# Two transformer blocks: score matmuls with all 128 rows, modulation in three MLPs, the softmax's factor on ScalarE

## The chip, the cores and the metric

The kernel runs on one core of one Trainium2 chip. The metric is the device time of one execution in microseconds. Three runs of the kernel before took 3540.41, 3541.93 and 3547.73 us; the median, 3541.93, is what a change is compared with. The engines are TensorE (PE in the profile, its weight loads PEld), VectorE (DVE), ScalarE (ACT), GpSimd (POOL) and SyncE (SP), which issues the DMAs.

## The reference

Two blocks of two layers each act on x, 512 tokens of 1024 channels, in float32. A layer of the first block, cut:

```python
u = rms_norm(h, attn_norm[l])
proj = u @ w_in[l]          # dq dk dv rq rk rv rg gq gk gv gate_logits
dq, dk = partial_rope(rms_norm(dq)), partial_rope(rms_norm(dk))
a = rms_norm(differential_attention(dq, dk, dv, lam), diff_subln[l]) * (1 - lambda_init)
r = silu(rg) * head_group_norm(bidirectional_retention(rq, rk, rv, ...))
gq, gk = axial_rope(rms_norm(gq)), axial_rope(rms_norm(gk))
c = grouped_query_attention(gq, gk, gv)
merged = sum over the three of sigmoid(gate) * (branch @ w_branch[l])
h = h + merged @ w_out[l]
h = h + square(relu(rms_norm(h, mlp_norm[l]) @ w_mlp_in[l])) @ w_mlp_out[l]
```

Differential attention has 4 heads, each with two softmaxes over 64 channels; the grouped attention has 8 query heads and 2 key heads of 64 channels. A layer of the second block, which also has a context stream ctx of 256 tokens:

```python
mx = split(silu_c  @ w_mod[l] + b_mod[l], 6)      # silu_c of c, for x
mc = split(silu_cc @ w_mod[l] + b_mod[l], 6)      # of c_ctx, for ctx
zx = (rms_norm(x, norm1_g[l]) * (1 + mx[1]) + mx[0]) @ w_in[l]   # zc from ctx alike
# queries of x (8 heads, 96 channels) attend to the 768 keys of ctx and x; in layer 0 ctx attends to its own 256
x = x + mx[2] * (concat(fourier, attention, conv) @ w_o[l])
x = x + mx[5] * (square(relu(modulate(rms_norm(x, norm2_g[l]), mx[3], mx[4]) @ w_mlp1[l])) @ w_mlp2[l])
# layer 0: the same for ctx with mc; layer 1: ctx is used for keys and values alone
return rms_norm(x, final_norm_g)
```

So of layer 1's modulation the context needs the first two of the six parts (columns 0 to 15 of 48 blocks of 128), and x all six.

## The kernel before

Activations lie transposed, 128 channels in the partitions and tokens in the free dimension, in tiles of 512 columns (256 for the context). Every operand of a matmul is split into a high part in fp32r and a low part, the rest, so a product is two or three matmuls (`mm3`, `gemm`). Weights come as blocks of 128x1024 (`wload`): SP loads one into a `raw` tile (3 of them), ScalarE writes the high part into a `w` tile, VectorE subtracts for the low part (`lo`, the rows `w<-raw,w`). There are 6 `w` tiles. The tag `r` holds 512-column fp32r tiles, 40 of them and some more in a phase (X1 in the first block's mixer).

The program runs phase after phase: for each of two layers of the first block the mixer (`mixer1`) and then the output projection and the MLP; then for each of two layers of the second block `mixer2` and its projection and MLP. In the trace of before the stretches are about 0 to 560 and 1000 to 1545 us for `mixer1`, 560 to 1000 and 1545 to 1965 for the first two MLPs, 1965 to 2260 and 2870 to 3140 for `mixer2`, 2260 to 2870 and 3140 to 3537 for the last two MLPs.

No code gives the order in which instructions stand in the engines' queues. `Sched` records the operations of a phase and then runs a list scheduler on them with a table of costs (`_cost`): each engine takes the ready operation with the smallest priority, which is its place in the record less a bonus (`sc.ahead`). A tile is taken when an operation starts and given back after its last reader. What comes out is a fixed order for each engine; the hardware works through each queue in order.

The scores of the first block (`scores`): the 64 channels of a query head lie stacked, the high part in one half of the partitions and the low part in the other (`stack_queries`). `stack_keys` writes the key's high part into both halves, with ScalarE and a copy on VectorE, and its low part into one half on GpSimd. The first matmul of a score tile then has 128 rows, high and low queries times high keys; the second has the 64 rows of the high queries times the low keys:

```python
mm(ps, q[m][:, a], k[0][m], True, False)
mm(ps, q[m][rows[m], a], k[1][rows[m]], False, True)
```

The softmax (`softmax`) takes the minimum on VectorE (the scores carry a minus sign), the exponential and its sum on ScalarE, and the reciprocal on VectorE. Then GpSimd multiplies the tile `e` by the reciprocal, TensorE transposes it, and ScalarE and VectorE split it into the parts for the product with the values. This stands three times: in `diff_attend` (of two softmaxes the first alone), `gqa_attend` and, for the second block, in `attend` inside `mixer2`.

The modulation vectors of the second block are computed beside the MLPs of the first (`side`, `modulation`). For each of 48 blocks of 128 outputs SP loads 128x1024 of the weights into an `mraw` tile (3 of them), and VectorE multiplies by the row silu(c) and sums, once for x and once for the context. Layer 0's 96 passes run in the first MLP, layer 1's 64 in the second. `mlp` calls `next(side)` after every second unit of its first half and after every unit of its second half; the scheduler may take these operations whenever tiles are free.

Of the kernel before, what the change touches and what calls it, by code (L numbers as in the profile page):

```python
# [21 lines left out]
D = 1024  # L22
T = 512
# [12 lines left out]
NRAW = 3  # L36
X1 = 8
X2 = 1
# [20 lines left out]
YADD = "V"  # L59
HALVES = 'P'  # L60
SWAP8 = list(range(8, 16)) + list(range(8)) + list(range(16, 32))
SWAP16 = list(range(16, 32)) + list(range(16))
# [69 lines left out]
class Op:  # L132
    __slots__ = ("eng", "calls", "cost", "prio", "idx", "bufs", "deps", "nexts", "ready", "unstarted", "soon", "allocs", "frees", "done", "rel", "outs", "port")

# [15 lines left out]
class Sched:  # L150


    def __init__(self, tc):
        self.tc, self.nc = tc, tc.nc
        self.tags, self.ops, self.bufs, self.bias, self.macro = {}, [], [], 0.0, None
        self.behind, self.dma, self.port = {}, 0.0, 0.0
        nc = tc.nc
        self.engines = {"PE": nc.tensor, "DVE": nc.vector, "ACT": nc.scalar, "POOL": nc.gpsimd, "SP": nc.sync}
# [60 lines left out]
    def ahead(self, n):  # L219
# [3 lines left out]
        self.bias = old  # L223

    def record(self, eng, name, a, k):
        call = (eng, name, a, k)
        if self.macro is not None:
            self.macro.append(call)
        else:
            self._add([call])  # L230

    def _add(self, calls):
# [16 lines left out]
        for b, r in writes:  # L249

            deps.update((o.idx, o) for o, q in b.written if starts or _meet(q, r))
            deps.update((o.idx, o) for o, q in b.read if _meet(q, r))
        op.deps = list(deps.values())
        op.prio = op.idx + self.bias
        op.allocs, op.frees = [], []
# [15 lines left out]
    def run(self):  # L271
# [44 lines left out]
        port = self.port  # L316
        events, order, now, dma = [(t, 0, 0) for t in sorted({0.0, *free_at.values()})], [], 0.0, self.dma
        for op in ops:
            if not op.done:
                if op.ready:  # L320
# [53 lines left out]
        while left:  # L374
# [30 lines left out]
            while events and events[0][0] <= now:  # L405
# [15 lines left out]
                for n in op.nexts:  # L421
                    n.done -= 1
                    n.ready = max(n.ready, now + lag(op, n))
                    if not n.done:
                        if n.ready <= now:
# [10 lines left out]
            while finished[low]:  # L436
                low += 1
            for t in self.tags.values():
                if t.blocked:
                    wake(t)  # L440
# [82 lines left out]
def kernel(  # L523
# [346 lines left out]
    def mixer1(l, mp, u):  # L870
# [86 lines left out]
        def stack_keys(x):  # L957

            out, l_ = [], sc.alloc("r")
            for r, o in zip(rows, reversed(rows)):  # L960
                k = sc.alloc("r")
                S.activation(k[r], x[r], AF.Copy)
                V.tensor_copy(k[o], k[r])
                lo(l_[r], x[r], k[r], G)
                out.append(k)
            return out, l_

        def scores(q, k, m, qt):

            a = slice(qt * P, (qt + 1) * P)  # L970
            ps = psum("sc")
            with sc.group():
                mm(ps, q[m][:, a], k[0][m], True, False)
                mm(ps, q[m][rows[m], a], k[1][rows[m]], False, True)
            return ps
# [61 lines left out]
        def diff_attend(hd, q, k, v, bo):  # L1037
            acc = psum("acc")
            for half in range(2):
                pt = [pair(T), pair(T)]  # L1040
                for j in range(2):
                    es = [sc.alloc("e") for m in range(2)]
                    r0, r1 = (softmax(scores(q, k, m, half * 2 + j), es[m]) for m in range(2))
                    V.tensor_tensor(out=r1, in0=r1, in1=neglam, op=ALU.mult)
                    G.tensor_scalar(out=es[0], in0=es[0], scalar1=r0, scalar2=0.0, op0=ALU.mult, op1=ALU.add)
                    V.scalar_tensor_tensor(out=es[0], in0=es[1], scalar=r1, in1=es[0], op0=ALU.mult, op1=ALU.add)
# [82 lines left out]
        def gqa_attend(i, q, k, v, out):  # L1129
            y = t32()  # L1130
            for m in range(2):
                acc = psum("acc")
                r = rows[m]
                for half in range(2):
                    pt = [pair(T), pair(T)]
                    for j in range(2):
                        e = sc.alloc("e")
                        rs = softmax(scores(q, k, m, half * 2 + j), e)
                        G.tensor_scalar(out=e, in0=e, scalar1=rs, scalar2=0.0, op0=ALU.mult, op1=ALU.add)
                        to_pt(e, pt, j)  # L1140
                        if j:
                            pv2(acc, v[m], pt, half)
                        yield
# [91 lines left out]

    mod = {(l, x): fixed(gp, 48, f"mod{l}{x}") for l in range(L) for x in "xc"}
    kept_c = {x: sc.fixed(dram.tile([P, D], F32, name=f"silu{x}")) for x in "xc"}

    def modulation(l):

        row = {}
        for i, x in enumerate("xc"):
            row[x] = sc.alloc("mrow")
            if l == 0:
                c, g = sc.alloc("mraw"), row[x]
                SP.dma_start(c, cc_d[i])
                S.activation(g, c, AF.Tanh, scale=0.5)
# [5 lines left out]
        yield  # L1253
        for j in range(48):
            who = "xc" if l == 0 or j < 16 else "x"
            raw = sc.alloc("mraw")
            SP.dma_start(raw, wmod_d[l, j])
            for x in who:
                out = raw if x == who[-1] else sc.alloc("junk")
                V.scalar_tensor_tensor(out=out, in0=raw, scalar=1.0, in1=row[x], op0=ALU.mult, op1=ALU.mult,  # L1260
                                       accum_out=mod[l, x][:, j:j + 1])
            yield
        for x in "xc":
            n = 48 if l == 0 or x == "x" else 16
            m = mod[l, x]
            V.tensor_tensor(out=m[:, :n], in0=m[:, :n], in1=vec[:, COL[f"bm{l}"]:COL[f"bm{l}"] + n], op=ALU.add)
            for at, g in ((8, f"n1{l}"), (32, f"n2{l}")):
                if at < n:
                    V.scalar_tensor_tensor(out=m[:, at:at + 8], in0=m[:, at:at + 8], scalar=1.0,
# [6 lines left out]
    def mixer2(l, mp, ux, uc):  # L1276
# [193 lines left out]
        def attend(v, y, par, si):  # L1470
# [5 lines left out]
            for hf in range(nq // 256):  # L1476
                pt = [pair(T) for _ in range(nk // 256)]
                for j in range(2):
# [261 lines left out]
    def side(l):  # L1740
        if l == 1:
            yield from context()
        yield from modulation(l)

# [42 lines left out]
    for l in range(L):  # L1787
        with phase(f"m2{l}", B2,
# [177 lines left out]
```

## Time and profile before

| | us |
|---|---|
| median of three runs | 3541.93 (3540.41 to 3547.73) |
| the profiled execution | 3539.29 |
| its span in the trace | 3537.5 |
| busy: PE, DVE, ACT, POOL | 3348.9, 2285.2, 1437.4, 948.2 |
| granted TensorE clock, mean | 0.977 of full speed |

The span is from the first to the last instruction of the program in one profiled execution; 1.8 us lie around it. Busy time is the time in which an engine has an instruction running; matmuls are pipelined, so that the length of one is longer than the time until the next can start. Nearly all operations are issued from one line of the kernel, so groups are told apart by the names of their tiles: `e<-sc,s` reads a score tile and writes an exponential. "issue" as what an engine waited for means nothing that the trace shows. The rows themselves stand in their own section below.

### The profile page before, as it was taken

How to read it: one execution, taken by the hardware profiler on the slowest of the kernel's cores; microseconds unless marked ns; L12 is line 12 of the kernel's file. 1: busy time of each engine (PE TensorE's matmuls, PEld its weight loads, DVE VectorE, ACT ScalarE, POOL GpSimd, SP SyncE). 2: the span in 40 equal slices, each digit the busy share in tenths (PEclk: the TensorE clock that was granted, in tenths of full speed). 3: DMA queues.
4: the chain of work that ended last, by engine and by line, in shares of the span. 5: the costliest groups of instructions: out<-in, count | busy, mean ns of one | idle time of the engine just before them, and what ended most of it. 6: DMA issues, size and time to landing. Idle time of an engine off the chain costs nothing.

```text
span 3537.5 us, 46905 instructions
## 1 busy us (share of the span) xinstructions
PE 3348.9 (95%) x17724; PEld 2823.5 (80%) x17724; DVE 2285.2 (65%) x4048; ACT 1437.3 (41%) x2699; POOL 948.2 (27%) x886
## 2 busy tenths in 40 slices
PE   6999999999989999999999987899999988889998
PEld 6787778788877877778888776788888886878887
DVE  7787866897378878668733898552332369963334
ACT  4554443322345544443223466441221334743233
POOL 4222323211132223231101565220210235621002
PEclk9999999999999999999999999999999998999999
DMA  3121124464321112154723210211111221022222
GB/s 125 60 69 60 66 72 173 154 213 162 110 97 55 69 66 72 66 179 159 270 99 104 69 37 1 84 60 59 61 68 58 69 79 50 19 84 96 96 96 84
DMA packets 100307, 324.48 MB, mean 92 GB/s; under 512 B 11120, under 2 KB 18288, under 8 KB 100080
## 3 DMA queue, kind: packets, MB, share of 16 engines
q1 hardware_dynamic: 100080, 321.48, 26.9%
q8 instruction: 139, 2.28, 0.3%
q14 instruction: 88, 0.72, 0.1%
HBM read 312.00 MB, written 9.44 MB: 91 GB/s over the span
## 4 chain that ended last, share of the span: by engine, by line
PE 85%; DVE 9%; ACT 3%; issue 2%; POOL 1%; DMA 0%; SPq 0%; DVEq 0%; ACTq 0%; POOLq 0%
PE mm L447 79%; PE sc L447 5%; DVE r L447 2%; DVE h L447 2%; PE acc L447 2%; DVE w L447 1%; DVE s L447 1%; DVE t L447 1%; ACT r L447 1%; ACT e L447 1%; DMA raw<-in_win_dram 0%; ACT t L447 0%; ACT w L447 0%; POOL t L447 0%; POOL h L447 0%
## 5 line engine op out<-in xcount | busy, mean ns | idle before, releaser
L447 PE MATMUL mm<-r,w 128*128 128x512 f32 (+1 forms) x12134 | 2570.7, 363 | 55.1 <-DVE w L447 23.0
L447 PEld LDWEIGHTS mm<-r,w 128*128 128x128 f32 x12134 | 2041.9, 191 | 399.7 <-DVE w L447 26.2
L447 DVE TENSOR_TENSOR w<-raw,w 128x1024 fp32r<-128x1024 f32 (+1 forms) x466 | 588.0, 1268 | 736.4 <-issue 358.1
L447 ACT ACTIVATE w<-raw 128x1024 fp32r<-128x1024 f32 (+1 forms) x466 | 483.7, 1046 | 1042.1 <-PE mm L447 900.8
L447 POOL TENSOR_SCALAR e<-e,s 128x512 f32<-128x512 f32 (+1 forms) x176 | 158.1, 901 | 397.6 <-DVE s L447 377.7
L447 ACT ACTIVATE e<-sc,s 128x512 f32<-128x512 f32 (+2 forms) x208 | 153.5, 739 | 131.5 <-DVE s L447 130.0
L447 PE MATMUL mm<-rc,w 128*128 128x256 f32 x768 | 166.1, 281 | 0.0
L447 DVE TENSOR_REDUCE s<-sc 128x1 f32<-128x512 f32 (+2 forms) x208 | 152.5, 741 | 19.3 <-PE sc L447 18.9
L447 PEld LDWEIGHTS mm<-rc,w 128*128 128x128 f32 x768 | 139.8, 189 | 20.3
L447 POOL TENSOR_TENSOR t<-t,t 128x512 f32<-128x512 f32 (+2 forms) x72 | 92.4, 1285 | 189.5 <-DVE t L447 162.9
L447 PE MATMUL mm<-r,r 128*128 128x256 f32 (+1 forms) x595 | 125.5, 343 | 11.5 <-DVE r L447 6.1
L447 DVE SCALAR_TENSOR_TENSOR mraw<-mraw,mrow 128x1024 f32<-128x1024 f32 x96 | 129.8, 1362 | 4.4 <-DMA mraw<-in_wmod_dram 3.1
L447 POOL TENSOR_TENSOR x<-t,x 128x512 fp32r<-128x512 f32 (+1 forms) x58 | 82.5, 1425 | 175.1 <-ACT x L447 175.1
L447 ACT ACTIVATE r<-mm 128x256 fp32r<-128x256 f32 (+1 forms) x278 | 98.0, 401 | 63.1 <-PE mm L447 60.0
L447 DVE SCALAR_TENSOR_TENSOR h<-cu,half,h 128x512 f32<-128x512 f32 (+1 forms) x144 | 122.6, 865 | 0.8
L447 DVE TENSOR_TENSOR r<-mm,r 128x256 fp32r<-128x256 f32 (+1 forms) x264 | 105.8, 433 | 22.0 <-ACT r L447 19.9
L447 ACT ACTIVATE r<-t 128x512 fp32r<-128x512 f32 (+3 forms) x141 | 84.2, 601 | 87.9 <-DVE t L447 66.0
L447 PEld LDWEIGHTS mm<-r,r 128*128 128x128 f32 x595 | 96.9, 202 | 25.8 <-ACT r L447 6.7
L447 PE MATMUL mm<-w,r 128*128 128x256 f32 x736 | 109.7, 290 | 7.3 <-DVE w L447 5.0
L447 ACT ACTIVATE t<-mm 128x512 f32<-128x512 f32 (+4 forms) x126 | 67.7, 538 | 119.6 <-PE mm L447 117.9
L447 PEld LDWEIGHTS mm<-w,r 128*128 128x128 f32 x736 | 98.3, 195 | 11.6 <-DVE w L447 5.3
L447 DVE TENSOR_TENSOR r<-t,r 128x512 fp32r<-128x512 f32 (+2 forms) x117 | 91.8, 791 | 13.1 <-ACT r L447 10.4
(596 smaller groups left out, 4124.2 us busy)
## 6 DMA issues: line engine op xcount, KB each, us to landing
raw<-in_wm_dram SPq DMA_DIRECT2D x256, 512.0 KB, 3.5
raw<-in_win_dram SPq DMA_DIRECT2D x134, 512.0 KB, 3.5
mraw<-in_wmod_dram SPq DMA_DIRECT2D x96, 512.0 KB, 4.4
raw<-in_wbr_dram SPq DMA_DIRECT2D x24, 512.0 KB, 3.5
raw<-in_wout_dram SPq DMA_DIRECT2D x16, 512.0 KB, 4.6
raw<-in_wo_dram SPq DMA_DIRECT2D x16, 512.0 KB, 3.5
kept<-h SPq DMA_DIRECT2D x24, 256.0 KB, 3.1
h<-kept SPq DMA_DIRECT2D x24, 256.0 KB, 5.4
```

The costliest lines, as they stand in the source:

```text
L447: getattr(self.engines[eng], name)(*[_real(x) for x in a], **{n: _real(x) for n, x in k.items()})
```

## The change

1. `stack_keys` writes the low part of a key into both halves, the second by a subtraction on VectorE, into one tile for each of the two heads in place of a common one. The second matmul of a score then takes all 128 rows, so that the low queries meet the low keys too. X1 goes from 8 to 9.
2. At three places the multiplication of `e` by the softmax's factor is a scaled copy on ScalarE in place of a tensor_scalar on GpSimd.
3. The modulation is spread over three MLPs: 32 of layer 0's 48 blocks in the first, the other 16 and layer 1's first 16 in the second, layer 1's other 32 (for x alone) in the third, where they go through the `raw` tiles of the weights. That phase gets an `mrow` tile and has 8 in place of 10 `rc` tiles. `paced(150)` tells the scheduler that such an operation may start only when all operations recorded up to 150 places before it are finished.

```diff
-X1 = 8
+X1 = 9
...
+PACE = 150
...
+        op.pace = 0 if self.pace is None else max(0, op.idx - self.pace)
...
+            while held and held[0][0] <= low:
+                op = ops[heapq.heappop(held)[1]]
+                heapq.heappush(events, (max(now, op.ready), 2, op.idx))
...
         def stack_keys(x):
-            out, l_ = [], sc.alloc("r")
+            out, lows = [], []
             for r, o in zip(rows, reversed(rows)):
-                k = sc.alloc("r")
+                k, l_ = sc.alloc("r"), sc.alloc("r")
                 S.activation(k[r], x[r], AF.Copy)
                 V.tensor_copy(k[o], k[r])
                 lo(l_[r], x[r], k[r], G)
+                lo(l_[o], x[r], k[r])
                 out.append(k)
-            return out, l_
+                lows.append(l_)
+            return out, lows
...
                 mm(ps, q[m][:, a], k[0][m], True, False)
-                mm(ps, q[m][rows[m], a], k[1][rows[m]], False, True)
+                mm(ps, q[m][:, a], k[1][m], False, True)
...
-                    G.tensor_scalar(out=es[0], in0=es[0], scalar1=r0, scalar2=0.0, op0=ALU.mult, op1=ALU.add)
+                    S.activation(es[0], es[0], AF.Copy, scale=r0)
...
-                        G.tensor_scalar(out=e, in0=e, scalar1=rs, scalar2=0.0, op0=ALU.mult, op1=ALU.add)
+                        S.activation(e, e, AF.Copy, scale=rs)
...
-                    G.tensor_scalar(out=e, in0=e, scalar1=rs, scalar2=0.0, op0=ALU.mult, op1=ALU.add)
+                    S.activation(e, e, AF.Copy, scale=rs)
...
-    def modulation(l):
+    def modulation(l, who, js, tag="mraw"):
...
-        for j in range(48):
-            who = "xc" if l == 0 or j < 16 else "x"
-            raw = sc.alloc("mraw")
...
+        for j in js:
+            with sc.paced(PACE):
+                raw = sc.alloc(tag)
...
     def side(l):
-        if l == 1:
+        if l == 0:
+            yield from modulation(0, "xc", range(32))
+        else:
             yield from context()
-        yield from modulation(l)
+            yield from modulation(0, "xc", range(32, 48))
+            yield from modulation(1, "xc", range(16))
...
-        with phase(f"p2{l}", {"mm": 7, "ms": 1}, (("t", XT, T, F32), ("rc", 10, T, F32R), ("hc", 8, TC, F32))):
+        with phase(f"p2{l}", {"mm": 7, "ms": 1}, (("t", XT, T, F32), ("rc", 8, T, F32R), ("hc", 8, TC, F32), ("mrow", 1, D, F32))):
...
-            mlp([wm12_d[l, m] for m in range(32)], [wm22_d[l, m] for m in range(32)], [(r, *v, n, mcols(l, x, 5)) for (r, x, n), v in zip(st, us)])
+            mlp([wm12_d[l, m] for m in range(32)], [wm22_d[l, m] for m in range(32)], [(r, *v, n, mcols(l, x, 5)) for (r, x, n), v in zip(st, us)],
+                iter(()) if l else modulation(1, "x", range(16, 48), "raw"))
```

VectorE's queue at the head of the first layer, before: the two copies of `stack_keys` (`r<-r`, 64x512), steps of a norm, and then the low half of the weight `w_104`, for which TensorE waits.

```order
L447 COPY r_72<-r_72 64x512
L447 COPY r_73<-r_73 64x512
L447 SCALAR_TENSOR_TENSOR s_133<-s_134,s_133 128x16
L447 TENSOR_TENSOR r_76<-t_121,r_75 128x512
L447 STREAM_TRANSPOSE t_122<-s_133 128x512
L447 TENSOR_TENSOR w_104<-raw_108,w_105 128x1024
```


And of the change, at the same place:

```order
L465 COPY r_71<-r_71 64x512
L465 TENSOR_TENSOR r_73<-t_119,r_71 64x512
L465 COPY r_72<-r_72 64x512
L465 TENSOR_TENSOR r_74<-t_119,r_72 64x512
L465 TENSOR_TENSOR t_117<-t_117,t_122 128x512
L465 TENSOR_TENSOR t_116<-mm_166,z_186 64x512
L465 TENSOR_TENSOR w_104<-raw_108,w_105 128x1024
```


Two subtractions of 64x512 (`r_73`, `r_74`) have come in behind the copies and stand ahead of the weight's low half.

ScalarE's queue at the first softmaxes of the second block (`e<-sc` is the exponential, `r<-mm` a high part of transposed weights or of another product, `k0h` a key), before:

```order
L447 ACTIVATE e_14079,s_129<-sc_14072,s_127 128x768
L447 ACTIVATE t_118<-mm_14075 128x512
L447 ACTIVATE t_119<-mm_14076 128x256
L447 ACTIVATE e_14080,s_133<-sc_14073,s_123 128x768
L447 ACTIVATE e_14081,s_125<-sc_14072,s_136 128x768
L447 ACTIVATE r_90<-mm_14074 128x256
L447 ACTIVATE k0h<-t_118 64x512
L447 ACTIVATE r_72<-mm_14077 128x2x128
L447 ACTIVATE r_67<-mm_14077 128x2x128
L447 ACTIVATE r_64<-mm_14075 128x2x128
```


And of the change:

```order
L465 ACTIVATE e_14040,s_129<-sc_14033,s_134 128x768
L465 ACTIVATE t_119<-mm_14036 128x512
L465 ACTIVATE t_120<-mm_14037 128x256
L465 ACTIVATE e_14040<-e_14040,s_123 128x768
L465 ACTIVATE e_14041,s_124<-sc_14034,s_131 128x768
L465 ACTIVATE r_91<-mm_14038 128x2x128
L465 ACTIVATE r_66<-mm_14038 128x2x128
L465 ACTIVATE r_99<-mm_14036 128x2x128
L465 ACTIVATE e_14042,s_128<-sc_14033,s_132 128x768
L465 ACTIVATE k0h<-t_119 64x512
L465 ACTIVATE r_81<-mm_14035 128x256
L465 ACTIVATE e_14041<-e_14041,s_137 128x768
```


The multiplications `e<-e,s` have come in two to six places behind their exponential, among the high parts.

VectorE's queue at the head of the first MLP, where the last residual sums (`h<-h,mm`) and the squares of the norm (`x`) stand, before:

```order
L447 TENSOR_TENSOR h_141<-h_141,mm_4415 128x512
L447 TENSOR_TENSOR h_143<-h_143,mm_4416 128x256
L447 SCALAR_TENSOR_TENSOR junk_4424,mod0x<-mraw_4419,mrow_4422 128x1024
L447 TENSOR_TENSOR h_144<-h_144,mm_4417 128x256
L447 SCALAR_TENSOR_TENSOR mraw_4419,mod0c<-mraw_4419,mrow_4423 128x1024
L447 SCALAR_TENSOR_TENSOR junk_4424,mod0x<-mraw_4420,mrow_4422 128x1024
L447 TENSOR_TENSOR h_146<-h_146,mm_4411 128x256
L447 SCALAR_TENSOR_TENSOR mraw_4420,mod0c<-mraw_4420,mrow_4423 128x1024
L447 TENSOR_TENSOR x_114<-t0x,x_112 128x256
L447 TENSOR_TENSOR x_111<-t2x,x_113 128x256
```


And of the change:

```order
L465 TENSOR_TENSOR h_141<-h_141,mm_4426 128x512
L465 TENSOR_TENSOR h_143<-h_143,mm_4427 128x256
L465 TENSOR_TENSOR h_144<-h_144,mm_4428 128x256
L465 TENSOR_TENSOR x_112<-t0x,x_113 128x256
L465 TENSOR_TENSOR h_146<-h_146,mm_4422 128x256
L465 TENSOR_TENSOR x_111<-t2x,x_114 128x256
```


The modulation passes (`junk` and `mraw`, writing mod0x and mod0c) are gone from between the sums.

## Rows read from the trace of the kernel before

**Rows 1.** The page: busy time by engine (part 1), then the chain by engine.

```profile
PE 3348.9 (95%) x17724; PEld 2823.5 (80%) x17724; DVE 2285.2 (65%) x4048; ACT 1437.3 (41%) x2699; POOL 948.2 (27%) x886
...
PE 85%; DVE 9%; ACT 3%; issue 2%; POOL 1%; DMA 0%; SPq 0%; DVEq 0%; ACTq 0%; POOLq 0%
```

**Rows 2.** Busy us by stretch (from:to, length, then engines): two plain MLP stretches.

```profile
640.00:975.00 335.00, 335.00 (x1556) 280.72 (x1555) 233.22 (x316) 104.72 (x143) 47.60 (x42) 1.00 0.50 164
...
2340.00:2870.00 530.00, 530.00 (x3137) 468.83 (x3137) 176.12 (x220) 131.93 (x229) 84.06 (x83) 1.00 0.19 64
```

**Rows 3.** The same, of the first mixer (two) and the second block's attention.

```profile
66.00:310.00 244.00, 242.74 (x1249) 194.46 (x1248) 190.85 (x378) 127.01 (x257) 64.91 (x58) 1.00 0.18 62
310.00:560.00 250.00, 242.99 (x1109) 188.75 (x1108) 183.90 (x367) 109.75 (x207) 74.78 (x60) 0.98 0.21 71
...
2075.00:2250.00 175.00, 136.42 (x930) 119.68 (x928) 155.09 (x354) 120.08 (x306) 98.11 (x109) 0.95 0.05 16
3000.00:3122.00 122.00, 104.03 (x754) 94.93 (x753) 110.00 (x228) 89.95 (x218) 70.32 (x67) 0.97 0.11 36
```

**Rows 4.** Timeline around one score pair: start us, length us, engine, instruction [idle before].

```profile
72.29 0.81 PE L447 MATMUL sc<-r,r 128*128 128x512 f32 x2
...
72.61 0.18 PEld L447 LDWEIGHTS sc<-r,r 64*128 64x128 f32 x1 [0.25 <-issue]
...
73.03 0.30 PEld L447 LDWEIGHTS mm<-w,r 128*128 128x128 f32 x2 [0.24 <-issue]
73.03 0.39 PE L447 MATMUL mm<-w,r 128*128 128x256 f32 x1
```

**Rows 5.** Timeline of TensorE around six plain matmuls of 512 columns.

```profile
303.14 1.55 PE L447 MATMUL mm<-r,r 128*128 128x512 f32 x6
304.52 0.28 PE L447 MATMUL mm<-w,r 128*128 128x256 f32 x1
```

**Rows 6.** Groups by form (xcount | busy us, mean ns | idle before): scores, first block.

```profile
L447 DVE TENSOR_REDUCE s<-sc 128x1 f32<-128x512 f32 x128 | 86.1, 681 | 18.8 <-PE sc L447 18.6
...
L447 PE MATMUL sc<-r,r 64*128 64x512 f32 x72 | 35.7, 496 | 0.0
...
L447 PE MATMUL sc<-r,r 128*128 128x512 f32 x72 | 31.3, 434 | 0.2 <-ACT e L447 0.2
...
L447 PEld LDWEIGHTS sc<-r,r 64*128 64x128 f32 x72 | 13.2, 183 | 21.5 <-issue 21.1 <-POOL r L447 0.4
```

**Rows 7.** Groups by form of VectorE: the 64x512 subtractions and copies.

```profile
L447 DVE CAST r<-r 64x512 fp32r<-64x512 f32 x18 | 20.0, 1114 | 1.0 <-ACT r L447 0.5
...
L447 DVE TENSOR_TENSOR r<-t,r 64x512 fp32r<-64x512 f32 x24 | 18.5, 772 | 2.0 <-ACT r L447 1.1
```

**Rows 8.** Timeline of VectorE and TensorE at the head of the first layer.

```profile
57.23 2.86 DVE L447 CAST r<-r 64x512 fp32r<-64x512 f32 x2
...
61.44 1.18 DVE L447 TENSOR_TENSOR w<-raw,w 128x1024 fp32r<-128x1024 f32 x1
...
62.68 0.58 PE L447 MATMUL mm<-w,r1x 128*128 128x256 f32 x1 [4.83 <-DVE w L447]
```

**Rows 9.** Groups by form of GpSimd: the multiplication by the softmax's factor.

```profile
L447 POOL TENSOR_SCALAR e<-e,s 128x512 f32<-128x512 f32 x96 | 80.8, 845 | 310.9 <-DVE s L447 304.9 <-ACT r L447 6.0
...
L447 POOL TENSOR_SCALAR e<-e,s 128x768 f32<-128x768 f32 x64 | 67.6, 1058 | 64.6 <-DVE s L447 58.0 <-PE mm L447 2.6 <-PE sc L447 1.8
...
L447 POOL TENSOR_SCALAR e<-e,s 128x256 f32<-128x256 f32 x16 | 9.8, 610 | 22.0 <-DVE s L447 14.8 <-ACT e L447 6.2 <-PE mm L447 0.8
```

**Rows 10.** Groups by form of ScalarE: copies in SBUF scaled by a column.

```profile
L447 ACT ACTIVATE h<-h,vneg 128x256 f32<-128x256 f32 x12 | 5.6, 499 | 3.8 <-DMA kept<-h 3.4 <-DVE vneg L447 0.3
...
L447 ACT ACTIVATE t<-cu,half 128x512 f32<-128x512 f32 x8 | 5.4, 709 | 0.0
```

**Rows 11.** TensorE's waits in the whole run: us in total, times, longest us.

```profile
PE mm L447 <- POOL e L447: 4.1, 5, 1.3
```

**Rows 12.** VectorE's modulation passes by form, and TensorE's longest wait in 560:640.

```profile
L447 DVE SCALAR_TENSOR_TENSOR mraw<-mraw,mrow 128x1024 f32<-128x1024 f32 x96 | 129.8, 1362 | 4.4 <-DMA mraw<-in_wmod_dram 3.1
...
PE mm L447 <- DVE w L447: 3.7, 1, 3.7
```

More of the change, by code (lines that the diff above doesn't have):

```diff
@@ L132 @@
 class Op:
-    __slots__ = ("eng", "calls", "cost", "prio", "idx", "bufs", "deps", "nexts", "ready", "unstarted", "soon", "allocs", "frees", "done", "rel", "outs", "port")
+    __slots__ = ("eng", "calls", "cost", "prio", "idx", "bufs", "deps", "nexts", "ready", "unstarted", "soon", "pace", "allocs", "frees", "done", "rel", "outs", "port")
 class Tag:
@@ L155, in __init__ @@
         self.tags, self.ops, self.bufs, self.bias, self.macro = {}, [], [], 0.0, None
+        self.pace = None
         self.behind, self.dma, self.port = {}, 0.0, 0.0
@@ L223, in ahead, with paced @@
         self.bias = old
+    @contextmanager
+    def paced(self, n):
+        self.pace = n
+        yield
+        self.pace = None
     def record(self, eng, name, a, k):
@@ L317, in run @@
         events, order, now, dma = [(t, 0, 0) for t in sorted({0.0, *free_at.values()})], [], 0.0, self.dma
+        held = []
         for op in ops:
             if not op.done:
-                if op.ready:
+                if op.pace:
+                    heapq.heappush(held, (op.pace, op.idx))
+                elif op.ready:
                     heapq.heappush(events, (op.ready, 2, op.idx))
@@ L424, in run @@
                     if not n.done:
-                        if n.ready <= now:
+                        if n.pace > low:
+                            heapq.heappush(held, (n.pace, n.idx))
+                        elif n.ready <= now:
                             heapq.heappush(ready[n.eng], (n.prio, n.idx))
@@ L1236 @@
     mod = {(l, x): fixed(gp, 48, f"mod{l}{x}") for l in range(L) for x in "xc"}
+    have_c = set()
     kept_c = {x: sc.fixed(dram.tile([P, D], F32, name=f"silu{x}")) for x in "xc"}
-    def modulation(l):
+    def modulation(l, who, js, tag="mraw"):
         row = {}
-        for i, x in enumerate("xc"):
+        for x in who:
             row[x] = sc.alloc("mrow")
-            if l == 0:
-                c, g = sc.alloc("mraw"), row[x]
-                SP.dma_start(c, cc_d[i])
+            if x not in have_c:
+                have_c.add(x)
+                c, g = sc.alloc(tag), row[x]
+                SP.dma_start(c, cc_d["xc".index(x)])
                 S.activation(g, c, AF.Tanh, scale=0.5)
@@ L1253, in modulation @@
         yield
-        for j in range(48):
-            who = "xc" if l == 0 or j < 16 else "x"
-            raw = sc.alloc("mraw")
[L1257 to L1261, printed above, removed]
+        for j in js:
+            with sc.paced(PACE):
+                raw = sc.alloc(tag)
+                SP.dma_start(raw, wmod_d[l, j])
+                for x in who:
+                    out = raw if x == who[-1] else sc.alloc("junk")
+                    V.scalar_tensor_tensor(out=out, in0=raw, scalar=1.0, in1=row[x], op0=ALU.mult, op1=ALU.mult,
+                                           accum_out=mod[l, x][:, j:j + 1])
             yield
[L1263 to L1266, printed above, removed]
+        for x in who:
+            m, a = mod[l, x], slice(js[0], js[-1] + 1)
+            V.tensor_tensor(out=m[:, a], in0=m[:, a], in1=vec[:, COL[f"bm{l}"]:COL[f"bm{l}"] + 48][:, a], op=ALU.add)
             for at, g in ((8, f"n1{l}"), (32, f"n2{l}")):
-                if at < n:
+                if at in js:
                     V.scalar_tensor_tensor(out=m[:, at:at + 8], in0=m[:, at:at + 8], scalar=1.0,
```

## The prediction

> **What bounds the kernel now.** I read the page first: TensorE is busy 95% of the span, and 85% of the chain that ended last lies on it [rows 1]. So a change pays if it takes work or idle time from TensorE, and other engines count only where TensorE waits for them. Then the busy time by stretch, because a mean over four stages hides their different limits. In the two plain MLP stretches TensorE is busy without a break, 335.00 of 335 us and 530.00 of 530, with VectorE at 70% and 33% [rows 2]. Nothing moved onto or off VectorE is worth anything there unless it makes TensorE wait. In the first block's mixer it is nearly the same: 242.74 of 244 us and 242.99 of 250, VectorE at 74 to 78%, ScalarE at 44 to 52% [rows 3]. Only the second block's attention is different: TensorE is busy 136 of 175 us and 104 of 122, VectorE 89% and 90%, ScalarE 69% and 74%, GpSimd 56% and 58%. There the engines wait for each other in turn.
>
> **The scores.** One score tile is two matmuls of 512 columns, the second with 64 rows. The timeline shows what this costs: the first starts at 72.29, the weight load of the 64-row one comes after 0.25 us idle, the load behind it after 0.24 us idle, and the next work on TensorE starts at 73.03 [rows 4]. The pair takes 0.74 us. Six plain 128-row matmuls of the same width, two operands in the same form, start at 303.14 and the next work at 304.52 [rows 5], 0.23 us each, 0.46 for two. The changed pair has 128 rows in both, so I expect 0.28 us less per pair. There are 128 score tiles of 512 columns [rows 6], so 128 x 0.28 = 36 us of TensorE's own time, 18 per layer. No wait hides it, since TensorE idles 1.3 of 244 us in the first of these stretches. The durations of the two forms, 496 and 434 ns [rows 6], would give only 0.06 us a pair, 8 us in all; but they are latencies that overlap the neighbours, and start to start is what the queue pays. The loads of the largest 64-row group stand 0.29 us each on the mean (21.1 us for 72, [rows 6]), which would make it 38. So 36, with 38 as the one end and 30 as the other, if a sixth is lost to a busier VectorE. What is late next is VectorE: 190.85 us [rows 3] in about 235 instead of 244 is 81%, still below the 89% that it reaches in the second block. I take 1 us back: **-35**.
>
> The Trainium skill speaks against this part. The row of its page "TensorE: Matmul & The Clock Gate" on small-K matmuls, under "Why this matters for your kernels", says that a lone matmul with few rows takes the same time as one with 128; by it the edit would save 0 and not 36. The two 0.24 us gaps around the 64-row load are the trace's answer [rows 4], and I go by them.
>
> **The keys.** stack_keys now writes the low half twice: one more VectorE subtraction of 64x512 per half, so 2 per call, 5 calls a layer, 20 in all at 772 ns [rows 7], 15 us of VectorE. The four calls a layer for the first attention lie beside TensorE work. The call at the head of each layer does not: TensorE already stands 4.83 us for a weight, whose low half comes on VectorE at 61.44, behind the two copies of stack_keys that start at 57.23 and take 2.86 us [rows 8]. The order of the change puts both new subtractions ahead of that weight. They cost 0.77 us each uncrowded, and up to 1.43 if they share with GpSimd as those copies (1114 ns mean, 2.86 for two) do. 1.5 to 2.9 per layer; I take 2, **+4** for both.
>
> **The softmax's factor.** 176 multiplications leave GpSimd, 96 of 512 columns, 64 of 768 and 16 of 256, at 845, 1058 and 610 ns [rows 9]. ScalarE's nearest rows, copies in SBUF scaled by a column, are 709 ns for 512 and 499 for 256 [rows 10]; the line through them gives 0.92 us for 768. In the first block this adds 48 x 0.71 = 34 us a layer to ScalarE's 237 of 494 [rows 3], some 57% of the shortened stretches. TensorE hides it: 0, with -4 (VectorE freed from GpSimd) and +6 (a queue of ScalarE that stands for the reciprocal) as ends.
>
> In the second block it is not hidden. The first layer adds 32 x 0.92 + 16 x 0.50 = 37 us to 120 of 175, which is 90%; the second 32 x 0.92 = 29 to 90 of 122, 98% [rows 3, 9, 10]. The multiplication itself is no slower than before (0.92 against 1.06), so a single softmax is not longer. But ScalarE's queue is in order: behind a factor that waits for VectorE's reciprocal stand the next exponentials and the high halves of the transposed weights, for which TensorE and VectorE wait. TensorE waits for GpSimd's multiplication only 4.1 us in the whole run [rows 11], so there is little to win. The busiest engine there now reaches 90%. If ScalarE reaches the same, the first layer's 157 us fit in 175 (0) and the second's 119 need 132 (+10). Against it, VectorE is no longer held by 77 us of GpSimd work, which may give back some 4. **+6**, ends -6 and +30.
>
> **The modulation.** The number of its VectorE passes stays 160 (1362 ns, [rows 12]); 32 move into the second block's first MLP, some come later in the first two. In the plain MLP stretches TensorE covers all: VectorE goes from 176 to 220 of 530 us in the one that gets more. At the start of the first MLP the order takes six passes out from among the residual sums and the norm. But TensorE's longest wait there is for a weight, 3.7 us [rows 12], not for a norm step, so I count **-1** (ends -4 and 0). The new DMAs go through the three raw tiles of the weights: 0, up to +5.
>
> **Sum.** -35 + 4 + 0 + 6 - 1 + 0 = -26. The profiled execution took 3539.3 us (span 3537.5), which gives 3513; the median of the three runs is 3541.9, 2.6 above it, which gives 3516. I say **3515**.
>
> **Rivals.**
> First, ScalarE becomes the bound in the second block. For it: 90% and 98% above. Against: work that can slip out of the window (weights, conv taps). If it reaches only 83% of the time, the 157 and 119 us take 190 and 144, +37 in place of +6: -35 + 4 + 37 - 1 = +5, 3547. Half of that growth gives 3528.
> Second, the far end of it, and the slower side: all new ScalarE time of the second block, 64 x 0.92 + 16 x 0.50 = 67 us, lands on the chain: -35 + 4 + 67 - 1 = +35, 3577. It decides from 32 us on, about half of the 67, where the gain of the scores is gone. Against: that chain runs mostly over TensorE and VectorE, and GpSimd's 77 us there were not on it either.
> Third, the rows do not matter: the 0.24 us gaps belong to something else in the pair, such as its operands or its place in the queue, and stay. 0 + 4 + 6 - 1 = +9, 3551. Against: six matmuls of the same width, accumulated in the same way, run without such gaps [rows 5], and what the pair has beside them is the 64 rows. The skill's row on small K, above, would come out here.
> Fourth, the modulation does slow the second block's first MLP: 32 pieces hold one of three weight tiles, and each makes TensorE wait as long as its pass, 32 x 1.36 = 44 us: 3515 + 44 = 3559. Against: no wait at all there now, 530 of 530.
> Fifth, all goes well: scores -38, keys +3, factors -4 and -6, modulation -4: -49, 3493.
>
> **How the numbers follow.** Forecast 0.62 (3503 to 3527). The first rival in its milder forms and in full 0.15, the larger part of it still faster; the second 0.04, the third 0.02, the fourth 0.03; the fifth 0.14. The range takes the forecast, two thirds of the fifth and the milder half of the first, 0.62 + 0.09 + 0.08, near 8 in 10: 3497 to 3535. 0.2% is 7 us, about what a measurement of this kernel can tell. Faster by more (below 3535): 0.62 + 0.14 + 0.08 = 0.84. Within: the other half of the first, 0.07. Slower: 0.04 + 0.02 + 0.03 = 0.09.
>
> **What would show it.** In the trace after, no score load with 64 rows, and pairs that take 0.46 us; the first block's two mixers about 17 us shorter each; the wait at the head of each layer near 7 us; the second block's attention at ScalarE above 85% and 0 to 10 us longer; the MLP stretches unchanged, TensorE without a break. I am wrong if the pairs keep their 0.74 us, if TensorE starts to wait for VectorE in the first block's mixer, or if the second block's two mixers grow by more than 30 us together.

## The result, and the profile after

The changed kernel takes **3487.44 us** (median of 4 runs, 3486.47 to 3494.29), the kernel before, run beside it, 3544.76 (median of 4, 3540.41 to 3547.73). The ratio is 0.9842, with an interval of 0.9827 to 0.9858: 56 us less, between 50 and 61. The forecast was 26 us less, the range ended at 3497, and the time lies 10 us below it. The sign was right, the size only half.

The sum was set on the profiled execution of before, 3539.29, and on a median of 3541.9; the median of the runs shown here is 5.5 and 2.8 us above them. Between the two profiled executions the span goes from 3537.5 to 3484.3, 53 us. The first two lines are the page of after, busy time and chain by engine; [rows 1] are those of before.

```profile
PE 3299.2 (95%) x17724; PEld 2819.1 (81%) x17724; DVE 2285.9 (66%) x4071; ACT 1540.8 (44%) x2875; POOL 796.4 (23%) x710
...
PE 82%; DVE 10%; ACT 5%; issue 2%; DMA 1%; POOL 0%; SPq 0%; DVEq 0%; ACTq 0%; POOLq 0%
```

TensorE has 49.7 us less busy time for the same 17724 matmuls. ScalarE gained 103.5 us and GpSimd lost 151.8, and the end of the kernel took no harm from ScalarE's gain.

**Where it went**, by start times of the same instruction in both traces, before and after. From the first score to the norm ahead of the MLP, the first block's mixer took 549.2 us and takes 526.6, a gain of 22.6, in layer 0. At the norm of the second MLP, the same point a layer later, the two traces are 46.7 us apart. From there to the last instruction only 6.5 more are won, 5.2 of them in the second block's first attention.

The scores first. These are TensorE's loads and matmuls for the largest score group of after, by form (xcount | busy us, mean ns | idle before), then TensorE's timeline around six score matmuls (start us, length us).

```profile
L465 PEld LDWEIGHTS sc<-r,r 128*128 128x128 f32 x144 | 26.1, 190 | 6.7 <-ACT e L465 2.0
...
L465 PE MATMUL sc<-r,r 128*128 128x512 f32 x144 | 41.6, 400 | 0.9 <-ACT e L465 0.9
```

```profile
299.97 1.53 PE L465 MATMUL sc<-r,r 128*128 128x512 f32 x6
301.34 0.61 PE L465 MATMUL mm<-r,w 128*128 128x512 f32 x2
```

The 64-row load with 21.1 us of idle time ahead of 72 instructions [rows 6] is gone: 144 loads now idle 6.7 us. These three score pairs take 301.34 - 299.97 = 1.37 us, 0.457 each, as the six plain matmuls did [rows 5]; the one pair shown of before took 0.74 [rows 4].

Busy time by stretch in after (from:to, length, then PE, PEld, DVE, ACT, POOL, then granted clock): two of the first mixer, the second block's first MLP, and the second block's two attentions. Those of before are [rows 3] and, for the MLP, [rows 2].

```profile
65.00:300.00 235.00, 233.33 (x1264) 197.00 (x1263) 192.45 (x381) 146.75 (x291) 38.57 (x27) 1.00 0.19 65
300.00:540.00 240.00, 231.67 (x1101) 189.11 (x1100) 192.36 (x375) 117.04 (x221) 64.18 (x43) 0.98 0.22 75
...
2290.00:2820.00 530.00, 530.00 (x3138) 468.84 (x3138) 217.15 (x287) 131.13 (x228) 89.36 (x82) 1.00 0.28 95
2029.00:2204.00 175.00, 139.16 (x948) 121.68 (x946) 154.96 (x364) 151.35 (x361) 55.63 (x60) 0.94 0.08 27
2947.00:3068.00 121.00, 101.54 (x753) 91.00 (x752) 103.22 (x228) 113.53 (x252) 36.97 (x36) 1.00 0.10 36
```

In the first mixer TensorE is still busy 99% and 97% of the stretches, with VectorE at 82% and 80%. In the MLP that took over 32 modulation steps TensorE has no gap, 530.00 of 530, with VectorE at 217 us. In the second layer's attention ScalarE is busy 113.53 of 121 us, 94%. That is more than the 90% that the forecast allowed it, and the attention did not grow: from its first score to the next norm it took 159.5 us and takes 158.7; in the first layer 234.0 and 228.8.

### The profile page after: what moved, and what is told of

The parts are those of the page before. It is cut to its first block, busy times and chain, and to the rows that moved or that the text cites. A ratio compares the mean times of both kernels' runs of the same rounds, so it can differ in the third digit from the quotient of the medians.

```text
span 3484.3 us, 46635 instructions
## 1 busy us (share of the span) xinstructions
PE 3299.2 (95%) x17724; PEld 2819.1 (81%) x17724; DVE 2285.9 (66%) x4071; ACT 1540.8 (44%) x2875; POOL 796.4 (23%) x710
## 4 chain that ended last, share of the span: by engine, by line
PE 82%; DVE 10%; ACT 5%; issue 2%; DMA 1%; POOL 0%; SPq 0%; DVEq 0%; ACTq 0%; POOLq 0%
PE mm L465 77%; PE sc L465 3%; DVE r L465 2%; DVE s L465 2%; ACT e L465 2%; DVE t L465 2%; DVE w L465 2%; PE acc L465 1%; DVE h L465 1%; ACT r L465 1%; ACT t L465 1%; DMA raw<-in_win_dram 1%; ACT w L465 0%; ACT q0h L465 0%; DVE e L465 0%
## 5 line engine op out<-in xcount | busy, mean ns | idle before, releaser
L465 PE MATMUL mm<-r,w 128*128 128x512 f32 (+2 forms) x12020 | 2538.9, 363 | 53.0 <-DVE w L465 20.4
L465 PEld LDWEIGHTS mm<-r,w 128*128 128x128 f32 (+1 forms) x12020 | 2022.6, 191 | 389.6 <-DVE w L465 25.3
L465 ACT ACTIVATE e<-e,s 128x512 f32<-128x512 f32 (+1 forms) x176 | 136.4, 786 | 15.9 <-DVE s L465 15.2
L465 ACT ACTIVATE r<-t 128x512 fp32r<-128x512 f32 (+2 forms) x137 | 80.7, 596 | 86.9 <-DVE t L465 59.4
L465 DVE TENSOR_TENSOR r<-t,r 128x512 fp32r<-128x512 f32 (+2 forms) x130 | 104.2, 806 | 14.9 <-ACT r L465 14.0
L465 PE MATMUL mm<-x,sums 128*128 128x512 f32 (+1 forms) x152 | 59.0, 409 | 35.3 <-ACT t L465 15.3
```

The source lines that it names most:

```text
L465: getattr(self.engines[eng], name)(*[_real(x) for x in a], **{n: _real(x) for n, x in k.items()})
```

## Experiments

Each ratio is to the kernel before in runs on the same chip (medians of before: 3545.45 for the first four, 3543.05 for the next four, 3542.56 for the next three, 3545.52 for the last).

**The parts, each alone.** First the scores with their keys (stack_keys with two low halves, X1 = 9, both matmuls with 128 rows); of the edit, the line of the second matmul.

```diff
-                mm(ps, q[m][rows[m], a], k[1][rows[m]], False, True)
+                mm(ps, q[m][:, a], k[1][m], False, True)
```

> The scores and stack_keys alone (X1 9, second low half, 128 rows), nothing else of the change. By the prediction: -35 for the pairs, +4 for the two heads, so -31 against the kernel before, 3514, and the wait at the head of each layer grows from 4.8 us to about 7. The rival after reading the trace of the change: pairs -37 and the heads no worse than before, because the order there moves other work too, so -37 to -40, 3507.

Measured: 3497.99, ratio 0.9871 (0.9854 to 0.9887), 46 us less. In its trace the norm of the second MLP, behind the first block's second mixer, comes 45.0 us earlier and the end 43.1: all of the gain lies in the first block's two mixers.

The factor on ScalarE, in the second block only and in the first only (the first block's other place is changed alike).

```diff
-                    G.tensor_scalar(out=e, in0=e, scalar1=rs, scalar2=0.0, op0=ALU.mult, op1=ALU.add)
+                    S.activation(e, e, AF.Copy, scale=rs)
```

> The factor on ScalarE in the second block alone (attend), the rest as before. By the prediction +6 (0 in the first layer, +10 in the second, less 4): 3551, with ScalarE above 85% in both attention stretches. Rival: GpSimd was the worse place because its multiplication waits behind other work on GpSimd and takes the memory port from VectorE, so -4 to -8: 3538.

> The factor on ScalarE in the first block alone (diff_attend and gqa_attend), the rest as before. By the prediction 0, ends -4 and +6, because TensorE covers it: 3545. Rival: the two tails of the first block, where the last softmaxes of the differential attention stand before the output projection, get shorter by some us each: -6 to -10, 3537.

Measured: second block 3536.45, ratio 0.9975 (0.9963 to 0.9986), 9 us less where 6 more were forecast; first block 3547.58, ratio 1.0002 (0.9992 to 1.0011), nothing, as forecast.

The modulation, spread over three MLPs and paced (cut).

```diff
-        for j in range(48):
+        for j in js:
+            with sc.paced(PACE):
```

> The modulation over three MLPs alone, with paced, the rest as before. By the prediction -1, ends -4 and 0 for the norms and up to +5 for the third MLP: 3544. Rival: in the trace of the change TensorE waits some 8 us less at the start of the first two MLPs, and this comes from the passes that no longer stand between the residual sums and the norm: -6 to -8, 3538.

Measured: 3539.86, ratio 0.9983 (0.9974 to 0.9992), 6 us less.

**What in the scores pays.** Keys alone: stack_keys as changed, the second matmul kept at 64 rows. Rows alone: 128 rows against the key tile that is there already, stack_keys unchanged; this kernel multiplies by the key's high parts a second time in place of the low ones, with the same number and size of instructions.

```diff
# keys alone (cut: stack_keys as in the change)
-                mm(ps, q[m][rows[m], a], k[1][rows[m]], False, True)
+                mm(ps, q[m][rows[m], a], k[1][m][rows[m]], False, True)
# rows alone
-                mm(ps, q[m][rows[m], a], k[1][rows[m]], False, True)
+                mm(ps, q[m][:, a], k[0][m], False, True)
```

> stack_keys as changed (second low half by VectorE, X1 9), but the second matmul of a score still with the 64 rows of the high queries, the rest as before; the added halves are written and not read. By the prediction the keys cost +4: 3549. Rival: the kernel with the scores alone came out some 9 us better than its pairs account for, because the record with these operations comes out in another order at the heads of the layers and in the differential attention; then this one is 3 to 9 us faster than before.

> The second matmul of a score with all 128 rows, stack_keys as before: it multiplies by the key's high parts a second time instead of the low ones (another result, the same work). This is the price of the rows alone. By the prediction 128 x 0.28 = 36 us, 38 at most; a pair takes 0.46 us. Rival: what the order of the keys gave belongs to the pairs (shorter waits behind them), so -42 to -46.

Measured: keys 3545.81, ratio 1.0012 (1.0000 to 1.0024), +4; rows 3498.53, ratio 0.9879 (0.9859 to 0.9900), -43 with an interval of -50 to -35. So the number of rows is what pays, and the third rival is dead. The +4 is weak: the interval starts at 0, one of the ten runs (3559.84) lies 6.6 us above the next, and with 128 rows in the pairs the keys cost nothing that shows (ratio 0.9871 with them, 0.9879 without).

In the trace of rows alone the norm behind the first mixer comes 21.1 us earlier, the one behind the second 42.2, and the end 42.9: that is 21 for each of the two mixers that hold the 128 pairs, and nothing elsewhere. The pair of [rows 4] now looks like this (TensorE, start us, length us); it takes 72.58 - 72.11 = 0.47 us in place of 0.74:

```profile
72.11 0.63 PE L447 MATMUL sc<-r,r 128*128 128x512 f32 x2
72.58 0.52 PE L447 MATMUL mm<-w,r 128*128 128x256 f32 x3
```

I split TensorE's time into the usual (median) distance from one matmul's start to the next and what goes beyond it. The first part falls by 38 us, 128 x 0.297, where a 64-row start stands 0.327 us behind a 128-row one and the next 0.424 behind it, against 0.227 each between 128-row ones. The other 5 are not shorter waits: TensorE's idle time in the whole is 188.6 us in before and 190.0 in rows alone. Part of them is in the pairs too. From the first start of a pair to the next work behind it, without the waits that fall in between, the 128 pairs add up to 101.0 us in before and 61.0 in rows alone, 0.79 and 0.48 each, 40 us less; the last 3 are not located. The median hides that in 47 pairs of before the 64-row matmul starts 0.41 to 0.45 us behind the first and not 0.327. Of these pairs 42 stand directly behind another pair. Two such pairs in a row, in before:

```profile
199.83 1.68 PE L447 MATMUL sc<-r,r 128*128 128x512 f32 x4
201.44 0.50 PE L447 MATMUL mm<-r1x,w 128*128 128x512 f32 x1
```

The two take 1.61 us, 0.81 each.

**Is ScalarE what the second block's attention waits for?** The change, and after each factor one or two more copies on ScalarE of 256 columns of the result into a tile that nobody reads.

```diff
                     S.activation(e, e, AF.Copy, scale=rs)
+                    for c in range(0, nk, 256):
+                        S.activation(spare, e[:, c:c + 256], AF.Copy)
```

> The changed kernel with extra work on ScalarE in the second block: after each softmax it copies e once more into a spare tile, 256 columns at a time, 112 copies in the first layer and 96 in the second at 0.33 to 0.42 us, some 38 and 33 us; nobody reads them. If ScalarE, at 88% and 94% of the two attention stretches, is what bounds them now: +55 to +70, 3545 to 3560. If the chain runs over all engines and ScalarE still has slack: +10 to +25.

Measured: 3552.59, ratio to before 1.0028 (1.0016 to 1.0040), so 65 us above the change. The two attentions of the second block from first to last score (columns as above):

```profile
2029.00:2218.00 189.00, 144.97 (x915) 125.76 (x913) 141.28 (x329) 174.42 (x442) 56.04 (x62) 0.90 0.03 11
2974.00:3111.00 137.00, 108.36 (x716) 95.68 (x714) 96.44 (x207) 129.36 (x315) 38.58 (x38) 0.91 0.03 9
```

The copies are 87.2 us of ScalarE (208 of 419 ns on the mean), and 65 of them come back as time. By attention (ScalarE's copies in the first and in the second):

```profile
L465 ACT ACTIVATE spare<-e 128x256 f32<-128x256 f32 x112 | 46.9, 419 | 0.2
...
L465 ACT ACTIVATE spare<-e 128x256 f32<-128x256 f32 x96 | 40.3, 420 | 0.2
```

From its first score to the norm behind it the first attention grows from 228.8 to 257.4 us, 29 for 47 of copies, and the second from 158.7 to 195.4, 37 for 40. ScalarE's share stands at 92% and 94%; in the change it is 86% and 94%. The first rival's mechanism is therefore real: in the second attention ScalarE has next to no slack left, and the change stands at that edge without having become longer; in the first some 18 us of copies still found room. The granted clock fell too, from 0.94 and 1.00 to 0.90 and 0.91, and how much of the 65 us belongs to that is not separated. The second rival, all 67 us of the new work on the chain, is dead: with the factor there the attentions take no longer than before.

**Is the first block's factor worth anything in the whole?** The change with that factor back on GpSimd in both places of the first block.

```diff
-                        S.activation(e, e, AF.Copy, scale=rs)
+                        G.tensor_scalar(out=e, in0=e, scalar1=rs, scalar2=0.0, op0=ALU.mult, op1=ALU.add)
```

> The changed kernel with the factor of the first block (diff_attend, gqa_attend) back on GpSimd. That part alone measured 1.0002, no difference. By the prediction (0) this is as fast as the change, 3487; if the shorter queue of GpSimd matters more once the pairs are short, it is 3 to 6 us slower; if ScalarE's queue does, 3 to 6 us faster.

Measured: 3484.83, ratio 0.9837 (0.9822 to 0.9852), the same as the change. Alone and in the whole it is worth nothing.

**Which half of the modulation?** Pacing with all 48 steps left where they were, and spreading with a pace so large that it holds nothing back.

```diff
# pacing alone (cut: layer 1's blocks likewise, none in the third MLP)
-            yield from modulation(0, "xc", range(32))
+            yield from modulation(0, "xc", range(48))
# spreading alone
-PACE = 150
+PACE = 1000000
```

(Both are shown against the modulation as changed.)

> The kernel before with the pacing alone: a modulation step may start only when all but the last 150 recorded operations ahead of it have ended; all 48 steps of each layer stay where they were. The modulation as a whole measured 6 us faster than before. Theory that the order at the start of the first two MLPs does it (VectorE's passes no longer among the residual sums and the norm): all of the 6 us, 3537 to 3541 beside 3545 for before. Theory that moving 32 steps out to the second block's MLPs does it: no change, 3544 to 3547.

> The kernel before with the modulation spread over three MLPs and no pacing. Theory that the pacing does it: no change, 3543 to 3547. Theory that the spreading does it: the whole 6 us, 3537 to 3541. If the passes still crowd the start of each MLP and now also of the third, it would be slower, up to 3550.

Measured: pacing 3534.18, ratio 0.9974 (0.9964 to 0.9984), -9; spreading 3544.24, ratio 1.0000 (0.9991 to 1.0009), 0. The pacing is all of it. TensorE's waits show where: around the start of the first MLP (560 to 640 us) and of the second (1545 to 1640 us), in before and then with pacing alone (us in total, times, longest us).

```profile
PE ms L447 <- DVE x L447: 3.2, 2, 1.6
...
PE ms L447 <- DVE x L447: 3.8, 2, 2.9
PE mm L447 <- DVE w L447: 2.1, 1, 2.1
```

```profile
PE mm L465 <- DVE w L465: 2.5, 1, 2.5
PE ms L465 <- DVE x L465: 1.0, 1, 1.0
...
PE ms L465 <- DVE x L465: 1.5, 2, 1.0
PE ms L465 <- ACT x L465: 0.8, 1, 0.8
```

The sums of the norm (ms) waited for VectorE's x for 3.2 and 3.8 us, and now 1.0 and 1.5; the wait for a weight goes from 3.7 [rows 12] to 2.5, and the one of 2.1 at the second MLP is gone. That is some 7 us of the 9. The same matmuls, counted from the program's start, stand 3.1 us further ahead behind the first of these starts than ahead of it, and 4.5 at the second; together that is the 7.6 us by which this trace is shorter.

**Why does the second block's factor gain?** The factor on ScalarE in the second block, as above, and GpSimd kept busy with multiplications of a spare tile that nobody reads.

```diff
                     S.activation(e, e, AF.Copy, scale=rs)
+                    for c in range(0, nk, 384):
+                        n = min(384, nk - c)
+                        G.tensor_scalar(out=spare[:, :n], in0=spare[:, :n], scalar1=rs, scalar2=0.0, op0=ALU.mult, op1=ALU.add)
```

> The factor on ScalarE in the second block only (measured 9 us faster than before), and GpSimd given other multiplications in its place, off every path: after each factor one or two of a spare tile (384 + 384, or 256 columns; by the lines of before some 0.73 us each, 64 x 1.46 + 16 x 0.61 = 103 us against the 77 that left GpSimd). Theory that the 9 us come from GpSimd's absence (VectorE no longer held by it): the 9 us go, 3543 to 3550. Theory that they come from the shorter or better ordered queues, GpSimd's work being no matter: they stay, 3534 to 3539.

Measured: 3549.73, ratio 1.0018 (1.0009 to 1.0027): the 9 us are gone and 6 lost on top, a swing of 15. The busy time from the first score of each attention to the norm behind it (columns as above), in before, then with the factor moved, then with GpSimd kept busy:

```profile
2074.00:2308.00 234.00, 194.24 (x1266) 170.92 (x1265) 173.53 (x384) 137.97 (x341) 108.99 (x125) 0.94 0.12 40
...
2996.00:3156.00 160.00, 142.03 (x967) 128.23 (x966) 125.55 (x246) 103.53 (x244) 81.33 (x81) 0.98 0.14 47
```

```profile
2078.00:2307.00 229.00, 192.32 (x1268) 169.02 (x1268) 169.22 (x384) 166.27 (x389) 66.27 (x75) 0.95 0.13 41
...
2994.00:3153.00 159.00, 139.62 (x965) 124.38 (x964) 118.47 (x247) 126.98 (x276) 47.02 (x49) 1.00 0.15 47
```

```profile
2076.00:2317.00 241.00, 197.76 (x1261) 172.45 (x1260) 173.50 (x383) 167.12 (x389) 121.89 (x157) 0.93 0.12 39
...
3004.00:3167.00 163.00, 145.38 (x966) 129.16 (x965) 122.11 (x247) 127.72 (x276) 91.67 (x113) 0.97 0.14 46
```

VectorE has nearly the same number of instructions in all three (630, 631 and 630). They take 299.1 us in before, 287.7 with GpSimd freed, and 295.6 with GpSimd busy on a tile that VectorE does not read or write there; the two share only the factor itself. TensorE's busy time goes the same way, 336.3, 331.9 and 343.1, and its granted clock too, 0.94 and 0.98, then 0.95 and 1.00, then 0.93 and 0.97. ScalarE has the new work in both of the last two. So the gain comes from GpSimd's absence. The other kept traces agree: in the eight whose attention is that of before the two attentions take 235.0 and 160.6 us on the mean and VectorE is busy 298 to 300 us in them; in the four with the factor on ScalarE and nothing added it is 229.0 and 158.7, 8 us less, and VectorE 287 to 288. Not settled is by which way most of it reaches the end: the spare multiplications also stand in GpSimd's queue ahead of its own work, and are 100 us against the 77 that had left; and whether the lower clock makes the longer attention or follows from it these runs don't tell.

**A version without the spreading.** The change with all 48 steps of each layer back in their places, pacing kept.

```diff
-            yield from modulation(0, "xc", range(32))
+            yield from modulation(0, "xc", range(48))
...
-            yield from modulation(0, "xc", range(32, 48))
-            yield from modulation(1, "xc", range(16))
+            yield from modulation(1, "xc", range(48))
```

> The changed kernel with the pacing kept and the spreading undone: all 48 modulation steps of each layer go where the kernel before had them. Measured alone, pacing with spreading gave 6 us, pacing without it 9, spreading without pacing 0. Theory that only the pacing pays: 3 us less than the change, 3482 to 3487 beside 3545 for before. Theory that the spreading pays once the pairs are shorter and VectorE is busier in the mixers: 3489 to 3497.

Measured: 3486.98, ratio 0.9837 (0.9824 to 0.9850). It is the same as the change; the 3 us between the two modulations alone don't show in the whole. No version that ran is measurably better than the change.

## Why the prediction reached only half of the gain

The parts measured alone give -43 + 4 + 0 - 9 - 6 = -54, against -56 measured in one (-50 to -61). With scores and keys measured together (-46, -52 to -40) it is -61. Either way the parts add up within the intervals, and the error lies in the terms.

**The scores, -35, measured -43 (-50 to -35).** The mechanism was right and the size a little low. The step was "36, with 38 as the one end", less 1 for VectorE. The step took one pair's 0.74 us for all 128, and that pair stood behind a plain matmul. On the mean a pair took 0.79 without its waits, more where it stood directly behind another pair, and 0.48 with 128 rows: 40 us. The "38 as the one end", from the idle time of the larger group of loads (0.29 us each, [rows 6]), was closer. The last 3 are not located, and the 1 us taken off for VectorE doesn't show. The interval does not part 38 from 43; the trace of rows alone, 42.9 us at the end, speaks for 43. The small-K row of the Trainium skill ("TensorE: Matmul & The Clock Gate", "Why this matters for your kernels") says that a single matmul of 32 rows takes the same time as one of 128; by it the edit would save nothing. It does not carry over to this sequence, where the measurement decides: a 64-row matmul between 128-row ones cost 0.3 us more than a 128-row one in its place.

**The keys, +4, measured +4 alone (0 to +8) and nothing beside the 128-row pairs.** This step failed too; that the number agrees is luck. I expected the wait at the head of each layer to grow from 4.83 us [rows 8] to about 7. In after it is 3.87 in the first layer and 3.65 in the second (4.97 in before): it shrank. These are VectorE and TensorE at the first head:

```profile
55.89 0.73 DVE L465 CAST r<-r 64x512 fp32r<-64x512 f32 x1
56.55 1.78 DVE L465 TENSOR_TENSOR r<-t,r 64x512 fp32r<-64x512 f32 x1
58.34 0.42 DVE L465 CAST r<-r 64x512 fp32r<-64x512 f32 x1
58.68 0.68 DVE L465 TENSOR_TENSOR r<-t,r 64x512 fp32r<-64x512 f32 x1
...
60.83 1.23 DVE L465 TENSOR_TENSOR w<-raw,w 128x1024 fp32r<-128x1024 f32 x1
...
62.12 0.58 PE L465 MATMUL mm<-w,r1x 128*128 128x256 f32 x1 [3.87 <-DVE w L465]
```

The two new subtractions do stand ahead of the weight and take 1.78 + 0.68 = 2.5 us, as I had it. But the first copy now starts at 55.89 and not 57.23, and the two copies take 1.15 us in place of 2.86, so the pass that writes the weight starts at 60.83 and not 61.44. I took the old start times as fixed; the order had moved them. If the keys cost 4 us, these arise elsewhere, and where is not shown.

**The factor in the first block, 0, measured 0**, alone and in the whole. TensorE covers it, as argued.

**The factor in the second block, +6, measured -9 (-13 to -5).** This is the step that failed. Its duration was right, as ScalarE's groups in after show:

```profile
L465 ACT ACTIVATE e<-e,s 128x512 f32<-128x512 f32 x96 | 68.3, 722 | 12.9 <-DVE s L465 12.4
...
L465 ACT ACTIVATE e<-e,s 128x768 f32<-128x768 f32 x64 | 59.7, 948 | 1.6 <-DVE s L465 1.5
...
L465 ACT ACTIVATE e<-e,s 128x256 f32<-128x256 f32 x16 | 8.4, 523 | 1.4 <-DVE s L465 1.3
```

722, 948 and 523 ns stand against 709, 920 and 499. The fault is in "The busiest engine there now reaches 90%. If ScalarE reaches the same, the first layer's 157 us fit in 175 (0) and the second's 119 need 132 (+10)." 90% was VectorE's share [rows 3], a share that was reached and not a limit, and I read it as one. ScalarE reached 94% of 121 us, and some 5 of its 119 us fell outside the stretch. Its idle time in before held slack. These are two of its waits in the first of the two attentions, for the transposes of the softmax and for the minimum ahead of the exponential (us in total, times, longest us), in before and with the factor moved alone:

```profile
ACT r L447 <- PE mm L447: 28.4, 27, 3.1
...
ACT e L447 <- DVE s L447: 12.9, 15, 1.7
```

```profile
ACT r L447 <- PE mm L447: 9.1, 9, 2.6
ACT e L447 <- DVE s L447: 3.7, 6, 1.6
```

The new work of that attention, 32 x 0.948 + 16 x 0.523 = 39 us, took the place of 28 us of such waits. On the other side, VectorE's relief was put at 4; with GpSimd freed VectorE lost 11 us of busy time, and the two attentions became 8 us shorter. The bounds of the term were -6 to +30, so even its best end was short of the truth.

**The modulation, -1, measured -6 (-9 to -3).** "TensorE's longest wait there is for a weight, 3.7 us [rows 12], not for a norm step": true of the longest wait, but the next in the same list, 3.2 us, was for the norm's sums, and at the second MLP, which I left out, they waited 3.8. The third MLP took its 32 steps without a gap, as forecast, so the fourth rival is dead.

Together: 8 us of the 30 that were missed lie in the scores, 15 in the second block's factor, 5 in the modulation, and the last 2 are within the interval. The fifth rival (all goes well, 3493) named the right parts and had a chance of 0.14; its scores (-38), second factor (-6) and modulation (-4) were each still a little short, its first factor (-4) was too much.

## What to carry to other kernels

Ask of an engine that gets more work how much of its idle time is slack. The share that another engine reached is no limit: here ScalarE went to 94% of a stretch at no cost, and only the run with extra copies showed that at this share nearly every further microsecond comes back (37 of 40). When a change takes work off an engine, also look for who gets faster beside it. Read a price from all instances of a pattern and not from one. And read the list of waits to its end at every repetition of a stage, not its longest entry at the first.

## What the runs showed of the hardware

A 64-row matmul of 512 columns between 128-row ones costs more of TensorE's queue than a full one: 0.327 us from the start before to its own (0.43 where the pair stands directly behind another), 0.424 to the next, 0.227 each for 128 rows. Giving it 128 rows saved 43 us in 128 pairs.

GpSimd multiplications that share nothing with VectorE but the factor went with longer VectorE work: in the second block's two attentions 630 instructions took 295.6 us with them, 287.7 without (631).
